# Moving the preparation of an S5 mixer from beside the experts to beside the attention

## The chip, the cores and the metric

The kernel runs on one core of one Trainium2 chip. A core has engines that each work through their own list of instructions in order: TensorE (PE, with its weight loads shown apart as PEld), VectorE (DVE), ScalarE (ACT), GpSimd (POOL) and SyncE (SP), which here does nothing but issue transfers (DMAs). An instruction that waits holds up all that stand behind it in its engine's list. The metric is the device time of one execution in microseconds (us). The kernel before took 3079.27, 3081.0 and 3085.3 us in three runs; their median is 3081.0 us.

## The reference: what is computed

Two blocks on 1024 tokens of 1024 features, in float32. The first block adds two branches (an RWKV-7 recurrence and a differential attention, each through its gate), then a mixture of 32 experts, then a per-layer embedding (PLE). The second block adds three mixers: SSD, HGRN-2 and S5.

```python
def first_block(x, p, norm_mix, w_in, ...):
    h = rms_norm(x, norm_mix[l])
    proj = h @ w_in[l]
    ...
    o_rwkv = rwkv7_branch(p_rwkv, ...)
    o_diff = diff_attention_branch(p_diff, ..., lambda_q1[l], lambda_k1[l], lambda_q2[l], lambda_k2[l], ...)
    mixed = (jax.nn.sigmoid(g_rwkv) * (o_rwkv @ w_branch_rwkv[l])
             + jax.nn.sigmoid(g_diff) * (o_diff @ w_branch_diff[l]))
    x = x + mixed @ w_out[l]
    x = x + hierarchical_moe(rms_norm(x, norm_ffn[l]), ...)
    ple_gate = jax.nn.sigmoid(rms_norm(x, norm_ple[l]) @ w_ple_gate[l])
    x = x + ple_gate * (p[l] @ w_ple_proj[l])
```

The S5 mixer is a diagonal complex state-space model: 32 groups of 16 channels with 64 complex states. What it makes of its parameters alone does not depend on x:

```python
    step = jnp.exp(log_step.astype(jnp.float32))[:, None]
    mag = jnp.exp(lr * step)
    ang = li * step
    ab_re, ab_im = mag * jnp.cos(ang), mag * jnp.sin(ang)
    ...
    bb_re = co_re[..., None] * b_re - co_im[..., None] * b_im
    bb_im = co_re[..., None] * b_im + co_im[..., None] * b_re
```

## The kernel before

The stages stand one after the other in the program: `branches` (the norm, the projections, the RWKV core, the attention, the gates), `mix` and `mix_out` (the gated sum and its product), `moe` (routing, then the experts one by one), `ple`, and `mixers` (the second block). A float32 product is made as three matmuls of rounded parts (hi x hi, lo x hi, hi x lo, lines L262 to L264); ACT (L181) and DVE (L182) make the parts. A scheduler at build time orders the instructions of each engine from the program and its own estimate of times, so instructions of neighbouring stages mix, but each engine then runs its list strictly in order.

Work that is to run beside other work is written as a Python generator, and the other stage calls `next` on it at given places. `proj_gate` is such a generator: 16 column blocks of gates, of which 5 are drawn before `diff_attn` and 11 inside it. `diff_attn` takes query blocks i = 1 to 7, then 0, and draws 13 times from its generator, spread evenly over the blocks. `moe` draws from its generator once an expert.

`s5_prep`, the first part of the S5 mixer's preparation, is a generator of 19 steps. Its first step issues on SP the loads of the parameters: `s_dcol` (L1681), the rows of lambda (L1686, L1687), `s_ls` for log_step (L1693, twice), `s_b` (L1696, real and imaginary part) and `craw` for c (L1701, eight loads of which two tiles are held at a time). Then PE transposes c (L1704), DVE makes the powers and coefficients (L1710 to L1790, short instructions on 16 columns), ACT takes exponentials and a sine (L1730 to L1751), and four last steps, one for each quarter of the groups, make outer products on DVE (L1633 to L1641), 16 small matmuls each on PE (L1806), and write `s5d_km` by ACT's queue. The element-strided loads are

```python
    nc.sync.dma_start(dcol[0:16], dap(ap["s5_d_2"], 0, [[1, 16], [16, 32]]))
    ...
        nc.sync.dma_start(ls[par * 64:(par + 1) * 64], dap(ap["s5_log_step_2"], par, [[0, 64], [2, 16]]))
```

They take 16 x 32 and 2 x 64 x 16 single float32 numbers from places that do not adjoin. Before, `s5_prep` runs beside the experts (expert 2 and after), and behind it `pp.late`, four products of PLE. `s5_scratch` (`d5`, L1890, L1891) fills `s5d_km` with zeros between `branches` and `mix`.

The start of the attention stands beside the end of the RWKV core. There the list of SP holds the loads of q and k by token tile (`qk`, L711, eight of them), `c_causal` (L137), the four vectors of lambda (`da_lam`, L694), RWKV's result going out (`d_or`, L608) and the load of v (`da_v`, L717). On DVE the state of the RWKV recurrence (`st`, L577) alternates with PE's product (L576); L696 makes lambda from `da_lam`; y, o (L586 to L607) end the RWKV core; L741 to L756 are the softmax. PE turns q and k (L715), multiplies them (L739), turns the weights (L762) and multiplies them with v (L767).

Of the kernel before, what the change touches and what calls it, by code (L numbers as in the profile page):

```python
# [11 lines left out]
F32 = mybir.dt.float32  # L12
# [16 lines left out]
def make_consts():  # L29
    """Constants that depend on shapes alone, one column block each of a [128, n] array."""  # L30
# [57 lines left out]
def flat(ap):  # L88
    """A contiguous DRAM array as one axis."""
    n = 1  # L90
    for s in ap.shape:
        n *= s
    return bass.AP(tensor=ap.tensor, offset=ap.offset, ap=[[1, n]])
# [6 lines left out]
class Parts:  # L100
    """A weight matrix split in hi + lo, in tiles of `part` blocks of 128 rows."""
# [9 lines left out]
class Kern:  # L111
# [19 lines left out]
    def const(self, *names, pool=None):  # L131
        """Load constants to SBUF tiles."""
        out = []
        for nme in names:
            o, n, rows = CONST_AT[nme]
            t = (pool or self.cpool).tile([rows, n], F32, name=f"c_{nme}")
            self.nc.sync.dma_start(t, self.cap[:rows, o:o + n])  # L137
            out.append(t)
        return out if len(out) > 1 else out[0]
# [26 lines left out]
    def bcast_row(self, pool, src, n, name, bufs=None):  # L166
        """A DRAM vector on every partition."""
# [4 lines left out]
    def rsqrt(self, out, v):  # L172
        """out = v ** -0.5, on [128, few]."""
# [5 lines left out]
    def split(self, hi, lo, src):  # L179
        """src as the sum of two float32r parts."""  # L180
# [3 lines left out]
    def norm_tile(self, pool, x, gain, out=None):  # L184
        """rms_norm of a token tile [128, 1024]."""
# [9 lines left out]
    def transpose_split(self, hi, lo, h, j, nk=8, k0=0, tag="t"):  # L195
        """Token tile j [128, nk*128] -> feature-major hi / lo [128, k, tokens]."""
# [11 lines left out]
    def load_w(self, pool, w, segs, kt=KT, raw_bufs=1, bufs=2, part=4):  # L208
        """Weight columns [kt*128, segs] -> float32r hi, lo, in tiles of `part` row blocks."""
# [18 lines left out]
    def resident_w(self, pool, w, k0, kt, cs, name, raw_bufs=2, gain=None, raws=None):  # L228
        """Row blocks k0..k0+kt-1 of w, columns cs -> Parts in one pair of tiles; a generator, a block at a time,
        that returns it. gain [128, kt]: a factor of every row; raws(k): a tile for the load of a block."""  # L230
# [17 lines left out]
    def finish(self, g):  # L248
        """What the generator g returns."""
# [9 lines left out]
    def mm3(self, out, a, b, first, last):  # L259
        """out += a^T b with a, b split in (hi, lo)."""  # L260
# [5 lines left out]
    def gemm_fm(self, w, c0, n, x, tok0, ntok=512, kt=KT, tag="mm"):  # L266
        """PSUM [n columns, ntok tokens] = (x @ w)^T for weight columns c0..c0+n."""
# [6 lines left out]
    def gemm_tm(self, w, x, j, n, kt=KT, c0=0, tok=None, tag="mm"):  # L274
        """PSUM [128 tokens of tile j, n columns] = x @ w."""
# [14 lines left out]
def rwkv_proj(K, hT, wp, xs_d, pool, order=RWKV_ORDER):  # L290
    """The projected columns after the token shift -> DRAM xs_d [1792, T], feature-major; the decay's part
    through tanh, the output gate's through sigmoid. hT: (hi, lo) of the normed input."""
# [29 lines left out]
def rwkv_core(K, xs_d, o_d):  # L322
    """RWKV-7 branch from its projections; o_d: DRAM [512, T], feature-major."""
# [14 lines left out]
    # by how long a unit needs their tiles  # L338
# [33 lines left out]
    # an array of 8 (pair of chunks, head) x 2 chunks, each [64, 64] and padded to 4160: the rows of one  # L372
    # parity, and the 16 x 16 blocks on all the diagonals (4 * 1040 = 4160)
# [7 lines left out]
    def unit(g, hf, carry):  # L381
        """A half of the tokens of two heads. A generator, that stops before what needs the inverse."""
# [6 lines left out]
        # log decay and its sums inside chunks of 64  # L389
# [13 lines left out]
        # kk = k * k_k, normalised per head  # L403
# [18 lines left out]
        # a, modified k, b = kk * a  # L422
# [7 lines left out]
        # [r~ | a~] and [b~ | k~] per chunk, and the chunk's decay  # L430
# [10 lines left out]
        # bonus: sum of r . k . r_k over a head, times v  # L441
# [7 lines left out]
        # token-major copies; the two chunks of a pair on the two halves of the partitions  # L449
        aP, lr = f4("aP", tag="aP"), f4("lr", tag="lr")       # [a~ | L_ak v], [b^ | L_rb^T]  # L450
# [6 lines left out]
        # scores, transposed: rows (chunk parity, s), per (pair of chunks, head)  # L457
# [14 lines left out]
        # X = (I - L_ab)^-1: 16-blocks by substitution, (chunk, head, block) on the partitions  # L472
# [17 lines left out]
        def blk(lhs, rhs, tag="a"):  # L490
            """Per (pair of chunks, head): lhs^T rhs on both halves, 64 columns."""
# [28 lines left out]
        ah = f4("ah", (128, 8, 128), "ah")     # [A^ | P^]  # L520
# [7 lines left out]
        # per chunk: [G^T | R'^T] and H, heads on the two halves  # L528
# [22 lines left out]
        # y inside the chunks  # L551
# [10 lines left out]
        # chain over the chunks  # L562
# [24 lines left out]
        # group norm per (token, head)  # L587
# [10 lines left out]
        # back to feature-major: (y * ln_w + ln_b + bonus) * g  # L598
# [27 lines left out]
def rope_tables(K, tab_d):  # L626
    """Rotary tables times the gains of q and k -> DRAM tab_d [2, 8, 128, 128]: cosines, signed sines."""
# [15 lines left out]
def proj_diff(K, hT, wp, pool, pd, beside):  # L643
    """The attention's columns -> DRAM pd [T, 1536]. beside(c): a generator of work beside a sixth of them."""
# [13 lines left out]
def norm_rope(K, pool, pd, tab_d, qk_d):  # L658
    """q and k of pd, normed and rotated -> DRAM qk_d [T, 1024]. A generator, by tiles of tokens."""
# [24 lines left out]
def diff_attn(K, qk_d, v_d, o_d, beside):  # L684
    """Differential attention. qk_d: norm_rope's; v_d: DRAM [T, 512]; o_d: DRAM [512, T], feature-major;
    beside: a generator of other work."""
# [4 lines left out]
    # lambda  # L691
# [29 lines left out]
    for i in (1, 2, 3, 4, 5, 6, 7, 0):  # L721
# [5 lines left out]
        # columns: by head, the reciprocals of the two sums  # L727
        rcs = wk.tile([128, 4, 2], F32, name=K.name("arc"), tag="arc", bufs=2)
        for h in range(4):
            # the two softmaxes: their columns of st are maxima, sums, by block of 512 keys  # L730
# [21 lines left out]
            # e0 / s0 - lambda e1 / s1 = (e0 - lambda s0 / s1 e1) / s0  # L752
# [37 lines left out]
def mix(K, o_ds, gate_d, mT):  # L790
    """The sum of the gated branches, feature-major, into mT, by token tile [128, (hi, lo), 8, 128].
# [1467 lines left out]
```

## Time and profile before

| | |
|---|---|
| median of the runs | 3081.0 us (3079.27 to 3085.3) |
| span of the profiled execution, first to last instruction | 3076.1 us |
| PE busy | 2897.0 us, 94% |
| DVE busy | 1965.6 us, 64% |
| ACT busy | 1319.5 us, 43% |
| mean granted clock of TensorE | 0.964 |

The profile is of one execution; its span lies 4.9 us below the median of the runs, which also count what lies around the first and last instruction. Matmuls are pipelined and their ends modelled, so that a PE that is busy through a stretch may still wait a little between matmuls. The granted clock is given as a share of full speed: 1.00 is 2.4 GHz and 0.50 is 1.2 GHz.

### The profile page before, as it was taken

Reading aid. Unit: us, or ns where it says so; the run is one execution under the profiler, and the core shown is the slowest. Engines: PE = TensorE matmul, PEld = TensorE weight load, DVE = VectorE, ACT = ScalarE, POOL = GpSimd, SP = SyncE. Lnnn points to the kernel's source line nnn. Section 1 sums busy time; section 2 is a strip of 40 time slices with the busy share of each in tenths; the row PEclk is TensorE's granted clock in tenths of the full one; section 3 lists DMA queues with packets and bytes.
Section 4 is the critical chain, followed back from the end, with each engine's and each line's share of the span. In section 5 each row is a group of like instructions: output and inputs, shape, how many; then the busy total and the mean of one; then the engine's idle time right before and its main releaser. Section 6 shows DMA issues by size and latency. Waiting matters only on the chain. (4 is left out here: it accounts for less than half of the span.)

```text
span 3076.1 us, 47278 instructions
## 1 busy us (share of the span) xinstructions
PE 2897.0 (94%) x18410; PEld 2400.8 (78%) x18410; DVE 1965.6 (64%) x3826; ACT 1319.5 (43%) x2167; POOL 231.9 (8%) x193
## 2 busy tenths in 40 slices
PE   6999999998998989889999997999999999999998
PEld 4888888775776867678777775878988999987776
DVE  4335778644454656679988786688546754548663
ACT  3222223213454222668777775444323343333341
POOL 0000111000000000012121110000000000000000
PEclk9999989997998998999999998999999999999999
DMA  5323333323114455799999995433344442137433
GB/s 162 115 89 82 102 116 107 101 65 106 62 62 144 152 187 195 247 339 378 370 347 335 319 346 212 138 105 95 102 129 128 133 133 74 55 106 232 125 124 127
DMA packets 378145, 503.30 MB, mean 164 GB/s; under 512 B 86039, under 2 KB 234422, under 8 KB 377918
## 3 DMA queue, kind: packets, MB, share of 16 engines
q1 hardware_dynamic: 347742, 458.63, 45.1%
q0 software_dynamic: 11296, 24.57, 2.2%
q10 hardware_dynamic: 18880, 17.05, 1.6%
q8 instruction: 146, 2.39, 0.3%
q14 instruction: 81, 0.66, 0.1%
HBM read 410.26 MB, written 106.68 MB: 168 GB/s over the span
## 5 line engine op out<-in xcount | busy, mean ns | idle before, releaser
L182 DVE TENSOR_TENSOR wh<-we,wh 128x1024 fp32r<-128x1024 f32 x384 | 452.8, 1220 | 72.3 <-ACT wh L181 70.3
L181 ACT ACTIVATE wh<-we 128x1024 fp32r<-128x1024 f32 x384 | 388.5, 1058 | 59.2 <-PE b L264 32.4
L262 PE MATMUL mm<-wh,hU 128*128 128x256 f32 (+1 forms) x768 | 253.3, 332 | 5.3 <-DVE z L1358 4.0
L263 PE MATMUL mm<-wl,hU 128*128 128x256 f32 (+1 forms) x768 | 251.8, 328 | 2.5 <-DVE wl L182 2.4
L264 PE MATMUL mm<-wh,hU 128*128 128x256 f32 (+1 forms) x768 | 250.0, 326 | 0.0
L264 PE MATMUL mm<-wh,hT 128*128 128x256 f32 (+1 forms) x640 | 215.1, 337 | 0.0
L262 PE MATMUL mm<-wh,hT 128*128 128x256 f32 (+1 forms) x640 | 207.0, 341 | 2.4 <-ACT ye L1060 2.3
L262 PE MATMUL mm<-hT,wh 128*128 128x512 f32 x480 | 196.5, 409 | 4.3 <-DVE edge L309 4.2
L182 DVE TENSOR_TENSOR wl<-wr,wh 128x1024 fp32r<-128x1024 f32 (+2 forms) x102 | 116.0, 1139 | 122.6 <-ACT wh L181 113.8
L264 PE MATMUL mm<-hT,wl 128*128 128x512 f32 x480 | 191.9, 400 | 0.0
L181 ACT ACTIVATE wh<-wr 128x1024 fp32r<-128x1024 f32 (+2 forms) x102 | 100.9, 992 | 211.3 <-PE mm L263 156.8
L263 PE MATMUL mm<-hT,wh 128*128 128x512 f32 x480 | 191.5, 399 | 0.0
L262 PEld LDWEIGHTS mm<-wh,hU 128*128 128x128 f32 x768 | 183.0, 239 | 9.6 <-DVE z L1358 5.0
L263 PEld LDWEIGHTS mm<-wl,hU 128*128 128x128 f32 x768 | 184.0, 240 | 5.8 <-DVE wl L182 3.5
L264 PEld LDWEIGHTS mm<-wh,hU 128*128 128x128 f32 x768 | 184.3, 240 | 1.4 <-issue 1.4
L262 PEld LDWEIGHTS mm<-wh,hT 128*128 128x128 f32 x640 | 125.0, 196 | 21.3 <-issue 4.3
L264 PEld LDWEIGHTS mm<-wh,hT 128*128 128x128 f32 x640 | 125.5, 196 | 12.6 <-issue 1.5
L262 PE MATMUL mm<-hU,wh 128*128 128x512 f32 x320 | 128.6, 402 | 4.5 <-ACT wh L181 4.5
L263 PE MATMUL mm<-hU,wh 128*128 128x512 f32 x320 | 127.3, 398 | 0.0
L264 PE MATMUL mm<-hU,wl 128*128 128x512 f32 x320 | 126.7, 396 | 0.0
L263 PE MATMUL mm<-wl,hT 128*128 128x256 f32 x384 | 115.8, 302 | 1.9 <-DVE wl L182 1.9
L262 PEld LDWEIGHTS mm<-hT,wh 128*128 128x128 f32 x480 | 92.3, 192 | 31.4 <-ACT xs L303 4.5
(704 smaller groups left out, 7098.1 us busy)
## 6 DMA issues: line engine op xcount, KB each, us to landing
we<-w_gate SPq DMA_DIRECT2D x64, 1024.0 KB
we<-w_up SPq DMA_DIRECT2D x64, 1024.0 KB
we<-w_down SPq DMA_DIRECT2D x64, 1024.0 KB
wr<-w_in SPq DMA_DIRECT2D x86, 512.0 KB
d_gate<-gz SPq DMA_DIRECT2D x32, 256.0 KB
gt<-d_gate SPq DMA_DIRECT2D x16, 512.0 KB
x<-d_x SPq DMA_DIRECT2D x16, 512.0 KB
dec<-sd_cum SPq DMA_DIRECT2D x16, 512.0 KB
```

The costliest lines, as they stand in the source:

```text
L181: self.nc.scalar.activation(hi, src, AF.Copy)
L182: self.nc.vector.tensor_sub(lo, src, hi.bitcast(F32))
L262: nc.tensor.matmul(out, a[0], b[0], start=first, stop=False)
L263: nc.tensor.matmul(out, a[0], b[1], start=False, stop=False)
L264: self.last = nc.tensor.matmul(out, a[1], b[0], start=False, stop=last)
```

## The change

Four edits. `s5_prep` is drawn inside `diff_attn`, two of its steps after every block of gates, through a new generator `both`; what is left of either is drawn behind the attention. Its pools of SBUF are taken from the right side. `s5_scratch` goes to the program's start. In `moe`, `pp.late` alone is left beside the experts, so that its products come with experts 2 and after instead of 21 and after. All else in the diff takes out comments and docstrings.

```diff
-def branches(K, x, xs_d, gate_d, or_d, od_d):
+def both(a, b, n):
+    for _ in a:
+        yield
+        for _ in range(n):
+            next(b, None)
+    yield from b
+def branches(K, x, xs_d, gate_d, or_d, od_d, prep):
...
-            diff_attn(K, qk_d, pd[:, 1024:1536], od_d, gates)
-            for _ in gates:
+            beside = both(gates, prep, 2)
+            diff_attn(K, qk_d, pd[:, 1024:1536], od_d, beside)
+            for _ in beside:
                 pass
...
-    branches(K, ap["x"][0], xs_d, gate_d, or_d, od_d)
     d5 = s5_scratch(K, dd)
+    branches(K, ap["x"][0], xs_d, gate_d, or_d, od_d, s5_prep(K, d5))
...
-    def beside():
-        yield from s5_prep(K, d5)
-        yield from pp.late()
-    moe(K, ring, x1_tiles, y_d, pp.early(), beside(), pp.weights)
+    moe(K, ring, x1_tiles, y_d, pp.early(), pp.late(), pp.weights)
...
-    pp = es.enter_context(K.pool(name="s5p", bufs=1))
+    pp = es.enter_context(K.pool(name="s5p", bufs=1, side="right"))
...
-    p0 = e0.enter_context(K.pool(name="s5b", bufs=1))
+    p0 = e0.enter_context(K.pool(name="s5b", bufs=1, side="right"))
...
-    with K.pool(name="s5c", bufs=1) as cp:
+    with K.pool(name="s5c", bufs=1, side="right") as cp:
```

SP at the start of the attention, before: the loads of q and k, the causal mask and the four vectors of lambda.

```order
L711 DMA qk_7509<-d_qk 128x1024
L711 DMA qk_7523<-d_qk 128x1024
L711 DMA qk_7537<-d_qk 128x1024
L137 DMA c_causal<-consts 128x128
L694 DMA da_lam<-lambda_q 128x64
L694 DMA da_lam<-lambda_k 128x64
L694 DMA da_lam<-lambda_q 128x64
L694 DMA da_lam<-lambda_k 128x64
L711 DMA qk_7551<-d_qk 128x1024
```

SP at the same place, in the changed kernel:

```order
L1681 DMA s_dcol<-s_d 16x32x1
L1686 DMA s_rows<-s_lambda_re 16x128
L1687 DMA s_rows<-s_lambda_im 16x128
L1693 DMA s_ls<-s_log_step 64x16x1 x2
L1696 DMA s_b<-s_b_re 128x16x16
L1696 DMA s_b<-s_b_im 128x16x16
L1701 DMA craw_7989<-s_c_re 128x1x64
L137 DMA c_causal<-consts 128x128
L694 DMA da_lam<-lambda_q 128x64
L694 DMA da_lam<-lambda_k 128x64
L694 DMA da_lam<-lambda_q 128x64
L694 DMA da_lam<-lambda_k 128x64
```

Eight loads of the preparation now stand between the third load of q and k and the mask, and lambda's vectors stand behind them.

DVE at the end of the RWKV recurrence, before: the state's steps (L577) and the making of lambda (L696).

```order
L577 TENSOR_TENSOR st_5401<-hh_5306,b_5407 128x64
L703 TENSOR_SCALAR da_subw<-pcol 128x1
L577 TENSOR_TENSOR st_5401<-hh_5306,b_5411 128x64
L577 TENSOR_TENSOR st_5401<-hh_5306,b_5415 128x64
L696 TENSOR_TENSOR da_lam<-da_lam 128x2x64
L577 TENSOR_TENSOR st_5401<-hh_5306,b_5419 128x64
L697 TENSOR_REDUCE da_lsum<-da_lam 128x2
L699 TENSOR_TENSOR da_lsum<-da_lsum 128x1
L701 TENSOR_SCALAR da_lsum<-da_lsum 128x1
L577 TENSOR_TENSOR st_5401<-hh_5306,b_5423 128x64
L577 TENSOR_TENSOR st_5401<-hh_5306,b_5427 128x64
```

DVE in the changed kernel, first the place where the preparation's arithmetic on `s_ls` begins, behind two of these steps of the state:

```order
L577 TENSOR_TENSOR st_5413<-hh_5318,b_5419 128x64
L703 TENSOR_SCALAR da_subw<-pcol 128x1
L577 TENSOR_TENSOR st_5413<-hh_5318,b_5423 128x64
L1710 TENSOR_SCALAR s_t_8159<-s_ls 128x16
L1711 TENSOR_SCALAR s_t_8159<-s_t_8159 128x16
L1712 SCALAR_TENSOR_TENSOR s_t_8160<-s_t_8159,s_ls 128x16
L1713 SCALAR_TENSOR_TENSOR s_t_8160<-s_t_8159,s_t_8160 128x16
```

and, thirteen short instructions of the preparation later, lambda and the next three steps of the state (the last one follows three rows on):

```order
L1716 TENSOR_TENSOR s_step<-s_step,s_t_8160 128x16
L1717 TENSOR_SCALAR s_step<-s_step 128x16
L696 TENSOR_TENSOR da_lam<-da_lam 128x2x64
L1716 TENSOR_TENSOR s_step<-s_step,s_t_8160 128x16
L577 TENSOR_TENSOR st_5413<-hh_5318,b_5427 128x64
L182 TENSOR_TENSOR wl_8014<-wr_8013,wh_8016 128x1024
L697 TENSOR_REDUCE da_lsum<-da_lam 128x2
L1717 TENSOR_SCALAR s_step<-s_step 128x16
L577 TENSOR_TENSOR st_5413<-hh_5318,b_5431 128x64
L1723 TENSOR_TENSOR s_step<-s_step,s_ni 128x16
L577 TENSOR_TENSOR st_5413<-hh_5318,b_5435 128x64
```

The making of lambda now stands behind the arithmetic on `s_ls`, and four steps of the state stand behind both, where three stood behind lambda alone (b_5419, b_5423, b_5427 above).

PE in the attention of query blocks 6 and 7, in the changed kernel, where the first quarter's small matmuls (L1806) stand between the transposes of the weights:

```order
L264 MATMUL mm_8943<-hT_97,wl_8910 128x512
L783 MATMUL t_8981<-c_ident,ao_8971 128x128 x4
L762 MATMUL t_9018<-c_ident,e_1398_8991 128x128 x4
L1806 MATMUL a_9083<-s_ca_8901,s_keep 16x128 x3
L1806 MATMUL b_9084<-s_ca_8901,s_keep 16x128 x2
L1806 MATMUL a_9083<-s_ca_8901,s_keep 16x128
L1806 MATMUL b_9084<-s_ca_8901,s_keep 16x128 x2
...
L1806 MATMUL b_9084<-s_ca_8901,s_keep 16x128
L762 MATMUL t_9024<-c_ident,e_1398_8991 128x128 x3
L1806 MATMUL b_9084<-s_ca_8901,s_keep 16x128
L767 MATMUL mm_9029<-da_v,attT_9017 128x128 x4
L762 MATMUL t_9065<-c_ident,e_1409_9038 128x128 x4
```

Before, these rows stood between the experts' matmuls; the three other quarters follow in the same blocks of the attention.

## Rows read from the trace of the kernel before

**Rows 1.** Timeline of POOL: each expert's scatter of its result; start, duration, idle before.

```profile
1293.01 0.99 POOL L1061 DMA_INDIRECT d_y<-ye,mo_tabi  x1 [15.38 <-ACT ye L1060]
1333.29 1.86 POOL L1061 DMA_INDIRECT d_y<-ye,mo_tabi  x1 [10.13 <-ACT ye L1060]
...
1496.53 1.02 POOL L1061 DMA_INDIRECT d_y<-ye,mo_tabi  x1 [0.78 <-ACT ye L1060]
...
1679.65 1.01 POOL L1061 DMA_INDIRECT d_y<-ye,mo_tabi  x1 [13.21 <-ACT ye L1060]
...
1784.87 1.02 POOL L1061 DMA_INDIRECT d_y<-ye,mo_tabi  x1 [0.30 <-ACT ye L1060]
...
1856.74 0.98 POOL L1061 DMA_INDIRECT d_y<-ye,mo_tabi  x1 [16.77 <-ACT ye L1060]
```

**Rows 2.** Timeline of SP's queue, 1283 to 1316 us: issues of loads.

```profile
1285.90 0.34 SPq L1681 DMA_DIRECT2D s_dcol<-s_d  x1
...
1287.37 3.58 SPq L1693 DMA_DIRECT2D s_ls<-s_log_step  x2
1291.05 1.99 SPq L1696 DMA_DIRECT2D s_b<-s_b_re  x1
1293.08 15.69 SPq L1696 DMA_DIRECT2D s_b<-s_b_im  x1
1308.81 3.54 SPq L1701 DMA_DIRECT2D craw<-s_c_re  x4
```

**Rows 3.** Transfers (DMA view) of 1293 to 1303 us.

```profile
DMA packets 1078, 0.00 MB, mean 0 GB/s; under 512 B 1078, under 2 KB 1078, under 8 KB 1078
```

**Rows 4.** Timeline of PE, 1310 to 1316 us.

```profile
1312.66 0.44 PE L1704 MATMUL t<-c_ident,craw 128*128 128x128 f32 x1 [13.59 <-DMA craw<-s_c_re]
```

**Rows 5.** Busy time by window, us and instructions by engine; then granted clock, DMA share, GB/s.

```profile
1293.01:1333.29 40.28, 23.14 (x94) 17.53 (x93) 16.80 (x21) 15.24 (x19) 2.04 (x3) 0.79 0.60 181
1496.53:1679.65 183.12, 179.49 (x885) 136.98 (x885) 162.68 (x185) 141.41 (x172) 41.09 (x18) 1.00 0.97 346
```

**Rows 6.** Timeline of SP's queue, 698 to 732 us.

```profile
698.56 1.27 SPq L711 DMA_DIRECT2D qk<-d_qk  x3
...
701.19 1.27 SPq L694 DMA_DIRECT2D da_lam<-lambda_q  x1
...
703.45 0.43 SPq L694 DMA_DIRECT2D da_lam<-lambda_k  x1
```

**Rows 7.** Timeline of DVE, 698 to 742 us.

```profile
703.42 0.22 DVE L577 TENSOR_TENSOR st<-hh,b 128x64 f32<-128x64 f32 x1 [2.27 <-PE b L576]
708.86 0.29 DVE L696 TENSOR_TENSOR da_lam<-da_lam 128x128 f32<-128x128 f32 x1 [5.22 <-DMA da_lam<-lambda_k]
709.07 0.21 DVE L577 TENSOR_TENSOR st<-hh,b 128x64 f32<-128x64 f32 x1
...
711.31 0.22 DVE L577 TENSOR_TENSOR st<-hh,b 128x64 f32<-128x64 f32 x1 [1.09 <-PE b L576]
```

**Rows 8.** Timeline of PE, 698 to 740 us: the first product with v.

```profile
738.82 1.19 PE L767 MATMUL mm<-da_v,attT 128*128 128x128 f32 x4 [0.94 <-DMA da_v<-d_pd]
```

**Rows 9.** Busy time by window: the start, the body and the end of the attention.

```profile
700.00:710.00 10.00, 4.39 (x60) 3.39 (x56) 1.28 (x7) 2.77 (x6) 0.00 (x0) 0.94 0.75 266
```
```profile
820.00:840.00 20.00, 20.00 (x112) 15.75 (x111) 9.86 (x30) 8.73 (x25) 0.00 (x0) 1.00 0.24 73
...
960.00:980.00 20.00, 15.94 (x95) 13.29 (x93) 7.43 (x32) 8.04 (x31) 1.01 (x1) 0.88 0.46 167
980.00:1000.00 20.00, 15.72 (x53) 11.22 (x53) 11.38 (x18) 10.89 (x22) 1.01 (x1) 0.70 0.93 326
```

**Rows 10.** Busy time of line L1806 alone: PE, PEld; clock, DMA share, GB/s.

```profile
1496.53:1679.65 183.12, 12.39 (x128) 6.46 (x128) 1.00 0.97 346
```

**Rows 11.** Lines of DVE in the experts' stretch: busy us, mean ns; one of six alike.

```profile
L1633 DVE TENSOR_TENSOR s_tmp<-s_keep 128x512 f32<-128x512 f32 x4 | 2.7, 686 | 0.0
```

**Rows 12.** Timelines at the attention's end: DVE, SP's queue, then PE.

```profile
970.21 0.86 DVE L1890 MEMSET s_zero<- 128x960 f32 x1 [3.40 <-PE mm L264]
```
```profile
971.10 0.35 SPq L1891 DMA_DIRECT2D s5d_km<-s_zero  x1
```
```profile
974.28 0.48 PE L739 MATMUL a<-da_kT,da_qT 64*128 64x128 f32 x2 [1.91 <-ACT e L748]
...
985.86 0.79 PE L262 MATMUL mm<-mx_oT,wh 128*128 128x512 f32 x1 [3.06 <-ACT wh L181]
```

## The prediction, made before the run

> **What bounds the kernel now.** I read the busy shares first: PE is busy 94% of the span, so the question in every stage is whether PE waits there, and for what. Then I followed the experts by the moment at which each scatters its result [rows 1]. From expert 25 to 29 nothing runs beside them: 1784.87 to 1856.74 us, 71.87 / 4 = 17.97 us each. That is the price of a clean expert. The preparation runs in the nineteen from 1293.01 to 1679.65: 386.64 us against 19 x 17.97 = 341.43, so it costs 45.2 us where it stands. The rows in between divide this: expert 2 takes 40.28, which is 22.3 over; the next nine take 163.24 against 161.7, 1.5 over; the last nine, with the quarters' outer products, take 183.12, 21.4 over.
>
> The 22.3 us are a wait. SP issues the preparation's loads from 1285.90, stays 15.69 us on the imaginary part of b and issues c only at 1308.81, 22.9 us after the first [rows 2]. In the ten microseconds from 1293 only 1078 packets arrive, together under 0.01 MB [rows 3]: those are the single numbers of `s_dcol` and `s_ls`, 16 x 32 + 2 x 64 x 16 = 2560 of them, and at 108 a microsecond 2560 need 23.7 us. All else on SP's queue stands behind them. PE, next in its list at the transpose of c, waits 13.59 us, until 1312.66, 26.8 us after the first issue [rows 4], and is busy only 23.14 of 40.28 us at a granted clock of 0.79 [rows 5]. The 21.4 us of the last nine are work: PE is busy 179.49 of 183.12 there, DVE 162.68 [rows 5].
>
> In the attention's body PE is as full, 20.00 of 20 us at full clock, but DVE has 9.86 [rows 9]. At its start it is otherwise: from 700 to 710 PE is busy 4.39 of 10 us, and what it waits for is the end of the RWKV recurrence, through DVE. DVE stands 5.22 us at L696 for lambda's vectors, with steps of the state behind it [rows 7]; PE's first product with v waits for the load of v, which SP issues behind RWKV's result [rows 8].
>
> **The change, part by part.**
>
> *Experts: -45.2.* All of the preparation leaves them. The four products of PLE that came behind it come at experts 2 to 6 instead; they are the same products in the same loop, and their input is loaded long ahead, so I cost that at nothing (a load that came late would be hidden by nothing, since PE is full). I keep -44 to -46 for the choice of clean experts.
>
> *The attention's start: +22.* The loads of the parameters are now on SP behind the third load of q and k, which ends at 698.56 + 1.27 = 699.83 [rows 6], and ahead of the mask and lambda. With the intervals of the experts the first load of c is issued at 699.83 + 22.9 = 722.7, and the mask and the four vectors by 725. In before lambda arrives 708.86 - 703.45 = 5.4 us after its last issue [rows 6, 7], so L696 starts near 730 instead of 708.86. The arithmetic on `s_ls` ahead of it waits for those same single numbers, but they land before lambda, so the later wait sets the time. Four steps of the state then stand behind L696: the three of before take 709.07 to 711.31 and one more adds about 1.2, so the last starts near 733.5 instead of 711.31: +22. Nothing covers it: y, o, RWKV's store, the load of v and the products with v hang on it in this order [rows 8], and the gates' matmuls that could fill PE stand further down its list. Low bound: the loads of b and c cost lambda nothing and only the single numbers do, 1303 - 1285.9 = 17.1 us to the end of the empty stretch [rows 2, 3], so lambda lands at 699.83 + 17.1 + 5.4 = 722.3, which with the extra step of 1.2 is +15. High bound: SP gets to the mask and lambda only when c has landed, at 726.6; with 2.7 us of issues (701.19 to 703.88 in before) and the 5.4, L696 starts near 734.7, +27.
>
> *PE in the attention: +16.* The matmuls of L1806 occupy PE 12.39 us in their 128 records [rows 10]; they go into a body in which PE is full. That is the low bound. The high bound is what all steps but the stalled first cost in the experts, 21.4 + 1.5 = 22.9. In between the difference is switching from one kind of matmul to another and DVE's share. DVE is at half there and at nine tenths in the experts [rows 5, 9], so I stay nearer the low end.
>
> *DVE and ACT: +2.* The 24 outer products of DVE are 0.686 us each [rows 11], 16.5 us, six together 4.1 us in front of the softmax. DVE has about 10 us in 20 free, so the free time hides them; a softmax that comes late costs PE what such waits cost elsewhere, 1.91 us at a time [rows 12]. Bounds 0 to 5.
>
> *Program's start and attention's end: +1 and -5.* The zeros (0.86 us on DVE, 0.35 us to issue, [rows 12]) move to the start of the program, in front of the first norm: 0 to +1.2. At the end of the attention they go, and SP is free earlier for what `mix` reads. There PE is idle 4.06 + 4.28 us in 960 to 1000 at a clock of 0.88 and 0.70 [rows 9], with 3.06 us before the first product of `mix` [rows 12]. The shifted list leaves PE more attention work behind the last gate. Bounds 0 to -8.3; I take -5.
>
> Sum: -45.2 + 22 + 16 + 2 + 1 - 5 = -9.2 us. Against the profiled span, 3076.1, that is 3066.9; the median of the runs lies 4.9 above the span, so 3071.8. By the low ends: -46 + 15 + 12.4 + 0 + 0 - 8.3 = -26.9, thus 3054; by the high ends: -44 + 27 + 22.9 + 5 + 1.2 - 0 = +12.1, thus 3093.
>
> **Rivals.** A measurement of this kernel can tell from no change what is over 0.2%, 6.2 us.
>
> *The stall at the start is short.* In the experts the single numbers were queued behind megabytes of weights; in the attention's start they are not. If that is why they were slow, lambda loses 5 us and not 22, and the sum is -26, 3055. For it: from 700 to 710 the DMA engines are not full, 0.75 [rows 9]. Against it: for ten microseconds the queue moved nothing else and still passed only 1078 packets [rows 3]. [...] I give it 0.16.
>
> *A wash.* The stall and the full price of the steps on PE, 22 + 22.9, give back what the experts win: 45 against 45, and the time stays within 6.2 us of 3081. It only needs the high end of the PE term: 0.23, with what else adds up to it.
>
> *The preparation stalls PE within the attention: slower.* PE takes its list in order, and prep's small matmuls (L1806) and transposes (L1704) now stand between those of the softmax. Each waits for DVE, whose list puts 4.1 us of outer products in front of softmax steps. If each of the 13 draws costs PE one wait like the 1.91 us for `e` [rows 12], the sum rises by 25 to +16: 3097. It decides from (9.2 + 6.2) / 13 = 1.2 us a draw. For it: the softmax is a chain over PE, DVE and ACT, and lateness in one link passes to the next. Against it: in the body PE is never seen waiting, with the gates' matmuls between [rows 9]. 0.20.
>
> The forecast itself, and what lies between it and the short stall: 0.41. So faster 0.57 (0.16 + 0.41), same 0.23, slower 0.20. The likeliest is 3072; its own range is 3054 to 3080. The range for 8 in 10 is 3050 to 3092: the short stall with a little more gain at the low end, the high ends' sum without its last us at the other.
>
> **What would show each step.** The scatters of experts 2 to 20 come 18 us apart, except for PLE's products at experts 2 to 6, 15.4 us in all (105.22 from 1679.65 to 1784.87 in before, less 5 x 17.97). SP stays some 15 us on `s_b` near 705 us, L696 on DVE starts near 730, and PE's first product with v near 761 instead of 738.82. In the attention's body the windows stay at 20 of 20 for PE, and the stage from the first product with v to the first product of `mix` is longer by 10 to 20 us. If L696 starts before 715, the term of the stall is wrong; if PE shows idle time before L1806, L1704 or L762 in the body, the third rival holds; if the experts still take over 18.5 us where no PLE product falls, the gain is not what I take it for.

## The result and the profile after

The changed kernel takes 3122.94 us (median of 4 runs, 3118.56 to 3126.29) against 3081.57 before: ratio 1.0137, 95% interval 1.0121 to 1.0153. It is 41 us slower, where 10 us faster was forecast, and outside the range. The spans of the profiled executions (first to last instruction) are 3116.8 and 3076.1, 40.7 apart. Six marks in the two traces divide this; a minus is time won:

| stretch | before, us | after, us | difference | forecast |
|---|---|---|---|---|
| start to the first load of q and k (L711) | 698.56 | 707.39 | +8.8 | +1 |
| from there to the last step of the state (L577) | 12.75 | 36.13 | +23.4 | +22 |
| from there to the first product with v (L767) | 27.51 | 27.52 | 0 | 0 |
| first to last product with v | 243.6 | 287.5 | +43.9 | +18 |
| from there to the first expert's scatter | 294.2 | 292.0 | -2.2 | -5 |
| first to last scatter | 608.2 | 571.8 | -36.3 | -45.2 |
| from there to the end | 1191.3 | 1194.4 | +3.1 | 0 |

Each trace is one execution. The mark of the first load moves by up to 9 us between traces of kernels whose list for PE is the same up to there (see the zeros, below), so the first row is exact to some us only.

The first and the last scatter of the experts, before and after:

```profile
1276.62 1.01 POOL L1061 DMA_INDIRECT d_y<-ye,mo_tabi  x1 [7.19 <-ACT ye L1060]
...
1884.77 1.68 POOL L1061 DMA_INDIRECT d_y<-ye,mo_tabi  x1 [7.23 <-ACTq L1094]
```
```profile
1350.53 1.01 POOL L1061 DMA_INDIRECT d_y<-ye,mo_tabi  x1 [7.41 <-ACT ye L1060]
...
1922.35 1.69 POOL L1061 DMA_INDIRECT d_y<-ye,mo_tabi  x1 [7.23 <-ACTq L1094]
```

The stall at the attention's start came as worked out. The timeline of SP's queue in the changed kernel, where [rows 2] and [rows 6] have the two halves of it:

```profile
707.39 1.27 SPq L711 DMA_DIRECT2D qk<-d_qk  x3
708.70 0.43 SPq L1681 DMA_DIRECT2D s_dcol<-s_d  x1
...
715.64 16.01 SPq L1696 DMA_DIRECT2D s_b<-s_b_im  x1
731.69 0.92 SPq L1701 DMA_DIRECT2D craw<-s_c_re  x1
...
734.58 0.43 SPq L694 DMA_DIRECT2D da_lam<-lambda_k  x1
```

From the preparation's first load (L1681) to the first of c (L1701) is 22.99 us, where the experts had 22.9. The DMA view of 716 to 726 us shows the same trickle as [rows 3]:

```profile
DMA packets 1078, 0.00 MB, mean 0 GB/s; under 512 B 1078, under 2 KB 1078, under 8 KB 1078
```

DVE's timeline, to be compared with [rows 7], and the window of 720 to 730 us, in which no engine does anything:

```profile
738.67 0.29 DVE L696 TENSOR_TENSOR da_lam<-da_lam 128x128 f32<-128x128 f32 x1 [3.68 <-DMA da_lam<-lambda_k]
...
743.52 0.22 DVE L577 TENSOR_TENSOR st<-hh,b 128x64 f32<-128x64 f32 x1 [0.97 <-PE b L576]
```
```profile
720.00:730.00 10.00, 0.00 (x0) 0.00 (x0) 0.00 (x0) 0.00 (x0) 0.00 (x0) 0.59 0.08 4
```

The attention's body is no longer the full stretch of [rows 9]. The line of L767 in the kernel before and in the changed one (durations, first and last start):

```profile
L767 PE MATMUL mm<-da_v,attT x288: 271/275/581, 738.8 to 982.4; 128*128 128x128 f32 x144
```
```profile
L767 PE MATMUL mm<-da_v,attT x288: 270/275/582, 771.0 to 1058.5; 128*128 128x128 f32 x144
```

PE's waits in it (what was waited for, us in all, times, the longest), first before from 738.8 to 984 us, then after from 771 to 1060:

```profile
PE b L739 <- ACT e L748: 3.0, 2, 2.4
PE a L739 <- ACT e L748: 1.9, 1, 1.9
PE t L783 <- DVE ao L780: 1.6, 1, 1.6
```
```profile
PE t L783 <- DVE ao L780: 6.1, 2, 3.5
PE t L783 <- DVE ast L744: 4.0, 1, 4.0
PE mm L767 <- ACT attT L763: 3.7, 6, 1.9
PE b L739 <- ACT e L748: 3.0, 2, 2.4
PE a L739 <- ACT e L748: 2.5, 2, 1.6
PE a L1806 <- ACT e L748: 1.7, 1, 1.7
```

How such a wait looks: PE's timeline in the changed kernel where query block 6 ends and the scores of block 7 begin. The small products (L1806) wait for ACT's L748, which reads the scores out of the PSUM buffers that they share, and the scores of the next head (L739) stand behind them; L783, which turns block 6's output, waits for DVE.

```profile
981.02 1.92 PE L1806 MATMUL a<-s_ca,s_keep 64*16 64x128 f32 x16 [1.74 <-ACT e L748]
982.87 1.12 PE L739 MATMUL a<-da_kT,da_qT 64*128 64x512 f32 x2
983.92 1.92 PE L1806 MATMUL b<-s_ca,s_keep 64*16 64x128 f32 x16
...
990.35 0.66 PE L783 MATMUL t<-c_ident,ao 128*128 128x128 f32 x4 [2.61 <-DVE ao L780]
```

What DVE does before that output (`ao`, L780): between L777, the first step of the output's norm, and L780 stand four of the quarters' outer products (L1634 to L1637), of which two are shown.

```profile
987.82 0.67 DVE L1635 TENSOR_TENSOR s_ca<-s_ca,s_tmp 128x512 f32<-128x512 f32 x1
...
989.03 0.67 DVE L1636 TENSOR_TENSOR s_tmp<-s_keep 128x512 f32<-128x512 f32 x1
989.63 0.67 DVE L780 TENSOR_TENSOR ao<-mm,aos 128x512 f32<-128x512 f32 x1
```

From L777 (985.46 us) to L780 it is 4.2 us here and 2.0 at the same block before; PE's wait is 2.61. The windows of query blocks 6 and 7, before and after, show the rest: the two take 83.7 us before and 113.3 after, PE is not full, and the mean granted clock of the last block is 0.88 instead of 0.96, so that more of it ran at the lower level of 1.2 GHz.

```profile
894.80:936.00 41.20, 40.98 (x219) 30.87 (x218) 22.82 (x54) 20.66 (x56) 1.01 (x1) 1.00 0.18 57
936.00:978.50 42.50, 38.50 (x217) 31.55 (x217) 18.48 (x55) 16.67 (x50) 1.01 (x1) 0.96 0.26 90
```
```profile
936.70:992.00 55.30, 50.25 (x287) 36.19 (x284) 33.52 (x77) 21.20 (x54) 1.01 (x1) 1.00 0.16 51
992.00:1050.00 58.00, 48.88 (x259) 38.02 (x258) 26.39 (x71) 26.54 (x70) 1.01 (x1) 0.88 0.41 147
```

From the first product with v to the first scatter, 537.8 us before and 579.5 after, PE's waits are 32 and 49 us in all, and the preparation's matmuls have taken 12 us that were not there. The remaining 12 or so are spread over the other lines, which cost more per matmul (L739 3.1 us in all, the gates' and mix's 5.4), at a mean granted clock of 0.92 instead of 0.94.

### The profile page after: what moved, and what is told of

It reads as the page before. It is cut to its first block, busy times and chain, and to the rows that moved or that the text cites. A ratio compares the mean times of both kernels' runs of the same rounds, so it can differ in the third digit from the quotient of the medians.

```text
span 3116.8 us, 47285 instructions
## 1 busy us (share of the span) xinstructions
PE 2903.1 (93%) x18410; PEld 2413.1 (77%) x18410; DVE 1968.4 (63%) x3826; ACT 1320.3 (42%) x2169; POOL 206.5 (7%) x193
```

## The experiments

The kernel before was timed again beside each group of these kernels; its median lay between 3078.3 and 3081.3, and each ratio is to the one beside it.

| kernel | us, median | ratio to before, 95% |
|---|---|---|
| c_before | 3059.05 | 0.9940 (0.9914 to 0.9965) |
| c_after | 3121.78 | 1.0131 (1.0098 to 1.0165) |
| no_prep | 3049.02 | 0.9903 (0.9872 to 0.9935) |
| zero_first | 3103.46 | 1.0089 (1.0054 to 1.0124) |
| z_mid | 3104.77 | 1.0085 (1.0069 to 1.0102) |
| z_mid_c | 3103.95 | 1.0079 (1.0063 to 1.0096) |
| a_pst | 3114.97 | 1.0118 (1.0101 to 1.0135) |
| a_noq | 3099.25 | 1.0068 (1.0044 to 1.0093) |
| a_nomm | 3111.97 | 1.0105 (1.0088 to 1.0122) |
| z_right | 3110.11 | 1.0093 (1.0076 to 1.0110) |
| c_pst | 3065.93 | 0.9956 (0.9940 to 0.9971) |
| all_fix | 3087.56 | 1.0021 (1.0010 to 1.0033) |
| a_pool | 3130.57 | 1.0172 (1.0148 to 1.0195) |
| c_pool | 3075.74 | 0.9998 (0.9986 to 1.0010) |
| all_pool | 3079.30 | 1.0002 (0.9988 to 1.0017) |

**The loads.** Two strided loads made whole, in the kernel before (c_before) and in the changed one (c_after):

```diff
-    nc.sync.dma_start(dcol[0:16], dap(ap["s5_d_2"], 0, [[1, 16], [16, 32]]))
...
+    drow, lraw = p0.tile([32, 16], F32, name="s5_drow"), f0("lraw", 32)
+    nc.sync.dma_start(drow, flat(ap["s5_d_2"]).rearrange("(r c) -> r c", c=16))
+    nc.sync.dma_start(lraw, dap(ap["s5_log_step_2"], 0, [[0, 128], [1, 32]]))
+    p = K.ps()
+    nc.tensor.transpose(p[:16, :32], drow, K.ident[:32, :32])
+    V.tensor_copy(dcol[0:16], p[:16, :32])
     for par in range(2):
-        nc.sync.dma_start(ls[par * 64:(par + 1) * 64], dap(ap["s5_log_step_2"], par, [[0, 64], [2, 16]]))
+        V.tensor_copy(ls[par * 64:(par + 1) * 64], lraw[par * 64:(par + 1) * 64, par:32:2])
```

> The kernel before, with the parameters' two strided loads made whole: s_d comes as 32 rows of 16 and is turned by PE, log_step as 32 numbers to every partition, of which two copies on DVE take every second. The 2560 packets of 4 bytes are gone, all else stays. If the wait at expert 2 is theirs (my theory), it goes, and of 3081.6 us some 22 are saved: 3059 us (3055 to 3064), expert 2 takes about 20 us instead of 40.3. Rival: SP's wait is for the 4096 packets of 64 bytes of b, then expert 2 stays near 40 and the time near 3080.

> The changed kernel with the same two loads made whole. Theory 1, three losses that stand by themselves (8 us upstream of the attention, 23 at its start by the single numbers, 42 between the first product with v and the first expert by the preparation's own instructions): the stall at the start goes, the rest stays, 3123 - 23 = 3100 us (3094 to 3106). Theory 2, the stall also spoils the order behind it, since the lists were made for a start without one: the stretch behind it shrinks from 579.5 us toward the 538 of the kernel before and its 12 us of small matmuls, and the time is 3065 to 3080.

In the kernel before it saved some 19 us (by the interval 11 to 26), and this is the fastest kernel that makes the whole result. SP's queue and POOL's scatter of expert 2 in c_before:

```profile
1284.13 2.41 SPq L1701 DMA_DIRECT2D s_b<-s_b_im  x1
```
```profile
1287.79 1.00 POOL L1061 DMA_INDIRECT d_y<-ye,mo_tabi  x1 [15.38 <-ACT ye L1060]
1313.45 1.85 POOL L1061 DMA_INDIRECT d_y<-ye,mo_tabi  x1 [13.28 <-ACT ye L1060]
```

The issue that held SP 15.69 us takes 2.41, and expert 2 takes 25.66 us instead of 40.28: 14.6 saved, where 20 us for the expert were expected. The other 7.7 us above a clean expert stay and were not traced further. The trace shows no more than these 14.6 as the loads' gain: its span is 17.1 shorter, of which 5.3 were already there at the first load of q and k, within what that mark moves by from one execution to another. In the changed kernel the same repair shortened the stretch from the first load of q and k to the last step of the state from 36.1 to 20.0 us, but the total did not move: the first load of q and k came 8 us later in that execution (715.18), and the products with v took 299.5 us instead of 287.5. Theory 2 fell; the adding up of theory 1 fell too.

**The whole preparation left out.** `no_prep` takes out the body of `s5_prep` and writes zeros for its tables; its S5 result is not made.

```diff
 def s5_prep(K, d):
...
+        nc.vector.memset(keep, 0.0)
+        nc.gpsimd.dma_start(d["keep"], keep)
     yield
```

> The kernel before with the preparation left out: its tables are zeros, s5d_km is zeros, nothing of it is loaded or computed. It shows what the preparation costs beside the experts in all. Theory: 45 us, so 3036 us (3032 to 3040), with experts of 18 us from the third on. Rival: the experts without it are held by something else (18.4 us each, as in a stretch of the changed kernel), then it costs 36 to 40 us and the time is 3042 to 3046.

From first to last scatter (1277.06 to 1847.24 us) 570.2 us are left of 608.2, so the preparation cost 38 us there and not 45: the rival's 36 to 40 held, though the time lies 3 us above its range. In no_prep six experts in a row take 110.30 us, 18.4 each:

```profile
1525.30 0.99 POOL L1061 DMA_INDIRECT d_y<-ye,mo_tabi  x1 [14.22 <-ACT ye L1060]
...
1635.60 0.99 POOL L1061 DMA_INDIRECT d_y<-ye,mo_tabi  x1 [14.39 <-ACT ye L1060]
```

By the runs' medians no_prep saves 29 us; its span is 30.4 shorter, since from the last scatter to the end it took 1198.5 us against 1191.3. That last stretch varies from 1190.6 to 1199.1 over the traces of these kernels, whose code is the same there.

**The zeros.** `zero_first` and `z_right` are the kernel before with the zeros at the program's start; `z_mid` is the changed kernel with them ahead of the attention.

```diff
+    d5 = s5_scratch(K, dd)
     branches(K, ap["x"][0], xs_d, gate_d, or_d, od_d)
-    d5 = s5_scratch(K, dd)
```
```diff
+            s5_zero(K, d5)
             beside = both(gates, prep, 2)
```

> The kernel before with s5_scratch alone moved to the program's start; the preparation stays beside the experts. If this move is what reorders the RWKV stage (theory 1: PE's waits at L410 for ACT, 16.7 us in all, and the first load of q and k 8.8 us later), the time is 3088 to 3092 us. Rival: the order there changes because the preparation is drawn in the attention, and the move alone leaves 3080 to 3083.

> The kernel before with the zeros of s5d_km first in the program, as in zero_first, but their tile on the other side of SBUF. The lists up to the attention then are a third order: L410 stands at row 1290 of PE instead of 1317 (1303 in zero_first), the next ones up to 160 rows earlier. If it is the order that costs, 10 to 25 us again, 3088 to 3103. If it is the tile, whose place the first stage takes over, the time is 3079 to 3083.

> The changed kernel with the zeros of s5d_km written just ahead of the attention instead of at the program's start; its list for PE up to the first product of the attention is then that of the kernel before, row for row. Theory: the move to the start alone costs what is lost upstream, so the first load of q and k comes at 698 us again instead of 707, the rest stays, 3114 us (3110 to 3118). Rival, from the zeros moved alone (+16 us at that place): it is worth 16 to 20, and 3103 to 3107.

One memset and one DMA at the start cost 0.9% on their own, with the tile on either side of SBUF; that is 25 and 29 us, more than either expectation had. What they change is the lists: up to the first load of q and k, PE's list of zero_first differs from that of before in 90 places, and that of z_right in 50. PE's wait there at L410, first in zero_first, then before; in the changed kernel it is 16.7 us in all:

```profile
PE t L410 <- ACT sq L407: 14.1, 3, 6.7
```
```profile
PE t L410 <- ACT sq L407: 0.7, 2, 0.4
```

How the wait comes about is seen in zero_first, on DVE and then on PE:

```profile
331.18 0.15 DVE L483 TENSOR_TENSOR pd<-xp,lp 64x1 f32<-64x1 f32 x1 [4.62 <-DMA lp<-ld]
...
332.42 0.41 DVE L391 TENSOR_SCALAR lo<-lo 128x512 f32<-128x512 f32 x1
```
```profile
337.16 1.87 PE L410 MATMUL t<-c_headsel,sq 128*128 128x2 f32 x8 [6.68 <-ACT sq L407]
```

DVE waits for a load at L483; the next unit's L391, which needs none of it, stands behind it; ACT waits for DVE, and PE, whose list now has L410 earlier (row 1303 instead of 1317), waits for ACT. In z_mid, whose list for PE up to there is that of before row for row, L410's wait is 0.6 us, the first load of q and k comes at 690.73 instead of 707.39, and its median is 18 us below the changed kernel's (16 by the ratios): the rival's number.

```profile
690.73 1.27 SPq L711 DMA_DIRECT2D qk<-d_qk  x3
```

The other traces bear this out. Nine kernels have L410 in the places that it has before, and their mark lies at 690.4 to 699.0 us, 695.7 on the mean; seven have it in the places of the changed kernel, and their mark lies at 707.4 to 715.2, 711.7 on the mean. So the move costs some 16 us up to here, and the +8.8 of the first two traces is a late execution of the one held against an early one of the other.

> The same, with the two strided loads made whole. Of the stall at the attention's start 16 of 23 us go (in c_after the last step of the state came 21.3 us behind the first load of q and k, against 37.3 in the changed kernel and 13.8 before). 3098 us (3093 to 3104) if the losses add up; near 3070 if the stretch behind the stall is better without it, which c_after already spoke against.

The load's repair does not pay in this place either: the stall is 12 us shorter than in z_mid and the products with v take 299.7 us instead of 290.2. In both pairs the products with v end at nearly the same distance from the first load of q and k, whatever the stall: 351.1 us in the changed kernel and 346.6 in c_after, 352.3 in z_mid and 346.5 in z_mid_c.

**Inside the attention.** Three kernels are the changed one with a part of the quarters taken off or moved: `a_noq` has no `for q in range(4)` at all, `a_nomm` makes the outer products and nothing behind them (in both `s5d_km` stays zero), and `a_pst` differs in one line, which takes PSUM buffers of the transposes' kind instead of the scores':

```diff
-            pk = [K.ps(tag="a"), K.ps(tag="b")]
+            pk = [K.ps(), K.ps()]
```

> The changed kernel without the four quarters (s5d_km stays zero): no outer products on DVE, no small matmuls, no writes of s5d_km. Loads, powers and coefficients stay. If the quarters cause the loss behind the stall (12 us of their own on PE, 17 of idle time, 12 by the clock), the stretch from the first product with v to the first expert is near 540 us again and the time 3083 us (3078 to 3090). If the short arithmetic of the earlier steps between the softmax's does, it is 565 us or more and the time 3108 or more.

> The changed kernel, where the quarters make their outer products on DVE but not the small matmuls nor what follows them (s5d_km stays zero). Without both, the stretch from the first to the last product with v took 255.3 us, with both 287.5. If DVE's outer products are what delays the softmax, it stays at 270 or more and the time at 3110 or more. If it is the matmuls with the buffers that they hold, it falls to 255 to 262 and the time is 3098 to 3106.

> The changed kernel, where the quarters' small products take PSUM buffers of the transposes' kind instead of the two kinds that the scores of the softmax use. If the quarters hold the scores' buffers and so keep PE from running ahead, the stretch from the first product with v to the first expert shrinks from 579.5 us by the 17 us of added idle time, and the time is 3106 us (3102 to 3110). If it is the order on PE and DVE, the time stays at 3119 to 3126.

The line of L767 in a_noq, a_nomm and a_pst:

```profile
L767 PE MATMUL mm<-da_v,attT x288: 271/275/581, 776.7 to 1032.0; 128*128 128x128 f32 x144
```
```profile
L767 PE MATMUL mm<-da_v,attT x288: 270/275/581, 769.9 to 1047.4; 128*128 128x128 f32 x144
```
```profile
L767 PE MATMUL mm<-da_v,attT x288: 271/275/582, 774.0 to 1049.9; 128*128 128x128 f32 x144
```

That is 255.3, 277.5 and 275.9 us, against 243.6 before and 287.5 after. The steps ahead of the quarters cost 11.7, the quarters 32.2 (21 to 24 by the times of the whole kernel; a_noq's lies 9 us above the range expected with this outcome). a_nomm came out as the first of its two outcomes, with 22.2 more than a_noq, but it is not the changed kernel less its matmuls: with nothing between them its 24 outer products all stand 64 to 83 us behind the first product with v, in the third query block, where the changed kernel has them in four groups, the last at 221.

The scores' buffers are worth 11.6 in this trace, two thirds of what was expected of them; by the medians it is 8, with intervals that overlap. z_mid_c and all_fix differ in this line alone and show it more clearly: the ratio falls from 1.0079 to 1.0021, and the products with v from 299.7 to 285.4 us.

```profile
L767 PE MATMUL mm<-da_v,attT x288: 270/275/582, 744.0 to 1043.7; 128*128 128x128 f32 x144
```
```profile
L767 PE MATMUL mm<-da_v,attT x288: 270/275/580, 745.0 to 1030.4; 128*128 128x128 f32 x144
```

Counted from the first product with v, the output of the third query block is done after 80 us before and after 84 in the changed kernel, that of the fourth after 116 and 126, of the sixth after 197 and 221, of the seventh after 240 and 279: the loss begins where the short steps stand and grows in the last two blocks, where most of the quarters' matmuls do. In a_noq it stays at 9 us from the fourth block to the seventh, and block 6 takes 41.5 us there with PE busy 41.28 of them, as before.

**DVE or not.** `a_pool`, `c_pool` and `all_pool` make the outer products on POOL, the changed kernel, c_before and all_fix otherwise being the same.

```diff
-            k.outer(nc, ca, k.c, q, 8, tmp, -1.0)
+            x_, p_ = k.pairs(q, 8)
+            G = nc.gpsimd
+            G.tensor_mul(tmp, x_[1], p_[1])
...
+            G.tensor_scalar(ca[:, 1], ca[:, 1], -1.0, None, op0=OP.mult)
```

> The changed kernel with the quarters' outer products on POOL (one more instruction each, for the sign). The products on DVE alone (a_nomm) held the attention 22 us longer than no quarters at all. If that is their place in DVE's list ahead of the softmax, the stretch from the first to the last product with v falls from 287.5 to 262 to 272 us, and the time to 3098 to 3108. If PE's wait moves on to POOL's slower products, or DVE is slowed by POOL, it stays at 280 or more and the time above 3114.

> The kernel before with whole loads and the outer products on POOL, beside the experts. Of c_before's 3059 us the quarters still hold about 12 (3059 against 3049 with no preparation at all). If they are DVE's, 3050 to 3055; if PE's own small matmuls, 3057 to 3062; if POOL's products hold up the experts' gathers and scatters, 3065 or more.

> The changed kernel with all three repairs and the outer products on POOL. If DVE's products are worth 15 to 22 us here too, 3066 to 3073, so faster than the kernel before by 8 to 15 us, but not than c_before. If not, 3083 to 3090.

a_pool is slower still, with 294.4 us from first to last product with v. The wait that is PE's largest in the changed kernel, 6.1 us there, has not gone:

```profile
PE t L783 <- DVE ao L780: 7.8, 2, 3.9
```

That taking the products off DVE gave nothing back does not show that DVE's time is harmless, for in this kernel they still stand in the way. They take POOL 35.2 us in this trace, where DVE needed 16.4, and DVE's other instructions between the first and the last product with v take 163.6 us together, where they took 152.7. The end of query block 6, on POOL and then on DVE, is to be held beside the timeline of 985 to 990 us above:

```profile
990.62 1.10 POOL L1810 TENSOR_TENSOR s_ca<-s_keep 128x512 f32<-128x512 f32 x1
991.67 1.04 POOL L177 TENSOR_TENSOR aos<-aos,mhalf 128x4 f32<-128x4 f32 x1
```
```profile
992.84 1.12 DVE L779 TENSOR_TENSOR aos<-aos,arc 128x4 f32<-128x4 f32 x1
...
994.49 0.68 DVE L780 TENSOR_TENSOR ao<-mm,aos 128x512 f32<-128x512 f32 x1
```

The outer products now stand before the attention's own step on POOL (L177), and L779 takes 1.12 us beside another of them, 0.14 in the changed kernel; from L777 to L780 it is 5.5 us. In all_fix the same move does pay: the products with v take 277.1 us in all_pool instead of 285.4, and most of the difference, 7.5 us, is there by the fourth query block; the ratio falls from 1.0021 to 1.0002, with intervals that just overlap. Beside the experts the same move costs 17 us, 3059 to 3076: by its time the last of the outcomes that were named for it; what waits there was not traced.

**All together.** `all_fix` puts the three edits shown into the changed kernel (zeros ahead of the attention, whole loads, the transposes' buffers); `c_pst` has whole loads and these buffers in the place beside the experts.

> The changed kernel with all three repairs: the zeros just ahead of the attention, whole loads, the quarters' products in the transposes' buffers. If the losses add up: 3104 less the 11.6 us that the buffers were worth, 3092 us (3087 to 3098), still slower than the kernel before. If it comes out below 3072, the place was good and its loads and buffers were not.

> The kernel before with whole loads (3059 us as measured) and the quarters' small products in the transposes' PSUM buffers. If the two buffers of the experts' products are what the quarters' 5 us each cost there, 3050 to 3055; if it is PE's own time, 3057 to 3061.

all_fix takes back 35 of the 41 us. With POOL for the products as well, the place beside the attention gives 3079 us, the time of the kernel before; the place beside the experts gives 3059 with the loads alone, and the buffers gain nothing there.

## Why the prediction was wrong

**The attention's start (+22) held in size, but not as a price to be added.** The stretch grew by 23.4 us, by the chain forecast: single numbers, lambda behind them, four steps of the state, RWKV's store, v. Yet where whole loads take 16 or 12 us of it away (c_after, z_mid_c), the products with v still end only 4.5 and 5.8 us earlier, counted from the first load of q and k, and the medians move by 1 us. That a stall there is paid in full was an assumption, and these pairs speak against it.

The rival of the short stall fell: the issue was held 16.01 us. The windows of [rows 3] and of 716 to 726 us have nothing else in flight in either kernel, so they do not compare the two places under a load. The DMA views of the 7 us ahead of them do, before and after:

```profile
DMA packets 1829, 1.58 MB, mean 223 GB/s; under 512 B 1043, under 2 KB 1075, under 8 KB 1828
```
```profile
DMA packets 1424, 1.54 MB, mean 212 GB/s; under 512 B 1023, under 2 KB 1055, under 8 KB 1423
```

Beside 1.5 MB of other loads more than 1000 small packets passed in 7 us (1285.9 to 1293, and 708.7 to 716); with nothing beside them 1078 needed 10. So the loads beside them were not what made them slow. The Trainium skill ("DMA: Bandwidth & Descriptors", "Latency and other measured facts") states that a lighter load on HBM makes a transfer's fixed cost smaller; the rate of these packets was not higher when the load was gone, and the fixed cost by itself is shown by no run here. It follows too that 108 packets a microsecond was not the rate of all 2560: that 2560 at this rate make 23.7 us, close to the 22.9 between the issues, is luck. The forecast used the 22.9.

**PE in the attention (+16) and DVE and ACT (+2) is the step that failed.** The bounds were PE's 12.4 us and what the same steps had cost in the experts, 22.9, plus at most 5 of waiting; 43.9 us were measured. The own time of the small matmuls was right, 12 us. Wrong was that the free half of DVE hides the rest. I had read a chain of softmax on four engines as a stretch bound by PE because the gates kept PE full; in the changed kernel PE waits 17 us more up to the first scatter, and the mean clock is 0.88 in the window of the last block. Shown are the share of the scores' PSUM buffers (11.6 us, 14.3 in the clearer pair), that of the quarters as a whole (32.2 in the traces, 21 to 24 in the times) and that of the steps ahead of them (11.7). For DVE's outer products the trace shows one wait, 2.61 us of PE at the end of block 6, behind four of them in DVE's list; what they cost in all no run separates.

The third rival had the place, PE's list in order and DVE's products in front of softmax steps. By the sign named for it, idle time before L1806, L1704 or L762, there is little: 1.7 us, none, and 1.5, where most of the waiting stands before L783 (10.1) and L767. Its +25 us meet the 26 that the attention cost beyond the forecast (43.9 less 18), but this is luck: it counted 13 equal waits, left out the buffers, and its 3097 still lies 26 us below the measured time, by the program's start and the experts.

**The program's start (+1) failed too.** I priced two instructions, 0.9 and 0.35 us, and not what their place does to the order of everything up to the attention: 16 to 18 us by z_mid, 16 by the marks of sixteen traces, 8.8 in the first pair. I had the reordered lists before me and gave their effect no term of its own.

**The experts (-45.2) were overrated by 7 to 9 us.** The yardstick of 17.97 us was taken from experts 25 to 29; with nothing beside them the middle experts take 18.4. The measured gain is 36.3 in the trace, 38 by no_prep. The attention's end gave 2.2 us, within its bounds of 0 to 8.3.

Left open: how the quarters' 32 us divide. The parts do not add up (11.6 to 14.3 for buffers, nothing to 8 for products moved to POOL, 22 for the same products bunched in one block), since each edit also makes new lists. Why whole loads shorten the stall and lengthen the products with v by nearly as much was not found. Why the scheduler's lists lose when two instructions come first was not settled beyond the waits shown.

## What to carry to other kernels

Here a stretch in which PE was full, because fillers lay between the links of a chain over several engines, had no room for more fillers that shared the chain's buffers and engines. Price what the chain loses, and not the engine's free share. Where a scheduler makes the lists, moving one instruction to the front may cost more than the instruction, so compare the order upstream, hold a term for it, and put such an instruction just ahead of its use, which gave back 16 to 18 us here. Do not read a cost of some us off one pair of traces at one mark: kernels with the same list for PE differed there by up to 9 us. And look first at why the work is dear where it stands: two loads made whole gave 19 us without moving anything.

## What was not expected of the hardware

With nothing else in flight, loads of single numbers passed at 108 packets a microsecond on SP's queue, in both places. An issue on SP behind some 4600 small packets (2560 of 4 bytes and, by the shape of b, 2048 of 64) was held for 16 us in both places, and for 2.41 us where the single numbers were gone. Eight transfers, some 314 KB in all by their shapes, so left four engines without one instruction for 10 us.

Moving 16.4 us of products from DVE to POOL took less than that off DVE: its other instructions became 10.9 us longer in the same stretch (152.7 to 163.6), 9.5 in all_pool (153.2 to 162.7).
